# RMSNorm with swish: framework waits, 2 MB transfers, and stores moved to a second issuing engine

## The chip, the cores and the metric

The kernel runs on one core of a Trainium2 chip; the other cores are idle. The metric is the device time of the program in microseconds (us), as the median of several executions. A profile gives the time line of one execution; its span is about 1.8 us shorter than the device time of the same execution (165.0 against 166.75 us before). Engines: ACT is ScalarE, DVE is VectorE, POOL is GpSimd, SP is SyncE, which only issues transfers here. A letter q after the name (SPq, ACTq) means the engine's sequencer, which issues DMA transfers and waits on semaphores. A semaphore is a counter on which an engine waits. A packet is one record of a DMA engine in the trace; a data packet here is 8 KB in a 1 MB transfer and 16 KB in one of 2 MB. A load or store of a tile has landed when the last of its sixteen completion events is recorded.

## The reference

```python
x = randn(16, 1024, 512)  # float32;  gamma = ones(512);  eps = 1e-5
rms = np.sqrt(np.mean(x ** 2, axis=-1, keepdims=True) + eps)
x_norm = x / rms * gamma
return x_norm * (1.0 / (1.0 + np.exp(-x_norm)))
```

The tensor has 16,384 rows of 2 KB, 33.6 MB. Each byte is read once and written once, 67.1 MB in all. There are 128 partitions, so the kernel holds 128 rows as "one row per partition"; four rows per partition are a piece of 1 MB.

## The kernel before

All waits are written by hand. SyncE issues both loads and stores, 1 MB each, in one program order: eight loads, and then a store and a load in turn. ACT makes three of four sums of squares and the swish, DVE the fourth sum and the normalization, POOL the power of -0.5. The cuts are marked.

```python
n = 4; n_act = 3; lead = 8; slots = 20          # T = 32 pieces of 1 MB
xb = pool.tile([P, slots, n, D], fp32, name="xb")
ld = [tc.alloc_semaphore(f"ld{s}") for s in range(slots)]
st = [tc.alloc_semaphore(f"st{s}") for s in range(slots)]
# ... ten more semaphores
def load(t):
    if t >= slots:
        nc.sync.wait_ge(st[t % slots], 16 * (t // slots))
    nc.sync.dma_start(out=X(t), in_=xv[t]).then_inc(ld[t % slots], 16)
def store(t):
    nc.sync.wait_ge(s_swish, t + 1)
    nc.sync.dma_start(out=ov[t], in_=X(t)).then_inc(st[t % slots], 16)
# ...
with tc.tile_critical():
    for t in range(lead):
        load(t)
    for t in range(T):
        store(t)
        if t + lead < T:
            load(t + lead)
    # ... ACT, DVE and POOL programs
    for s in range(slots):                       # the closing waits
        nc.sync.wait_ge(st[s], 16 * ((T - 1 - s) // slots + 1))
```

## Time and profile before

The time is 166.93 us, the median of three runs (166.81 to 167.04).

| what | value | how to read it |
|---|---|---|
| DMA, one queue | 97.0% of 16 engines | the sixteen DMA engines are nearly never idle: they bind |
| ACT, DVE busy | 120.5 us, 112.0 us | of 165.0 us: neither binds |
| rate in mid-span | 427 GB/s | 67.1 MB at that rate take 157 us |
| first transfer issued, first data | 0.94 us, 1.95 us | from the trace |
| last landing | 162.47 us | the last store's completion |
| end of the program | 164.97 us | 2.50 us after the last landing |

From the page of the kernel before: the span, the DMA share and the rate in 40 equal slices of 4.1 us, and the queues (packets, MB, share of 16 engines' span).

```profile
span 165.0 us, 713 instructions
...
DMA  4999999999999999999999999999999999999990
GB/s 157 415 425 429 425 342 429 411 431 427 427 431 419 431 423 433 423 431 425 429 427 427 423 425 431 421 435 419 435 423 431 425 425 431 421 433 423 433 405 26
...
q1 hardware_dynamic: 9216, 67.11, 97.0%
q14 instruction: 5, 0.04, 0.1%
```

DMA stands at 9 tenths from the second slice to the last but one. (In the tables below the DMA share can come out just above 1, for the recorded times of the packets are added up.) The one slice with 342 GB/s is where the first stores meet the loads.

The table by stretches of the kernel before. The columns are: stretch and length in us, busy us of DVE, ACT and POOL (with counts), clock, DMA share, GB/s.

```profile
20.00:22.00 2.00, 1.89 (x6) 2.00 (x5) 0.66 (x1) 1.00 0.97 360
22.00:24.00 2.00, 2.00 (x4) 2.00 (x6) 0.78 (x1) 1.00 0.92 324
...
60.00:80.00 20.00, 14.04 (x28) 15.38 (x31) 5.76 (x4) 1.00 1.01 427
...
155.00:159.00 4.00, 0.00 (x0) 0.00 (x0) 0.00 (x0) 1.00 1.01 426
159.00:161.00 2.00, 0.00 (x0) 0.00 (x0) 0.00 (x0) 1.00 0.91 385
161.00:163.00 2.00, 0.00 (x0) 0.00 (x0) 0.00 (x0) 1.00 0.06 25
163.00:165.00 2.00, 0.00 (x0) 0.00 (x0) 0.00 (x0) 1.00 0.01 4
```

So some 4 us pass at the end in which almost nothing moves. The view of the output tensor's transfers gives the last store's start (152.3 us) and the shortest time to landing (10.2 us), which belongs to that last store: it landed at 162.5 us.

```profile
L79 SPq DMA_DIRECT2D out_dram<-xb x32: 332/344/348, 15.3 to 152.3; - x32
...
DMA to landing us min/median/max: 10.2/22.4/24.0
```

### The profile page before, as it was taken

What the parts mean: (1) busy time and instruction counts of PE and PEld (TensorE: products, weight loads), DVE (VectorE), ACT (ScalarE), POOL (GpSimd) and SP (SyncE); (2) the same over time, 40 slices, a digit from 0 to 9 for tenths busy, and PEclk for the clock granted to TensorE, in tenths of its full rate; (3) what the DMA queues carried; (4) which work ended last, traced back from release to release, by engine and by line L of the source; (5) the groups of instructions that cost most, each with busy time, mean ns of one, the idle gap of its engine ahead of it and who ended that gap; (6) DMA issues with size and microseconds to landing.
All of it is one profiled execution on the core that took longest, in us unless ns stands there. A gap on an engine that the chain in (4) does not pass through costs nothing.

```text
span 165.0 us, 713 instructions
## 1 busy us (share of the span) xinstructions
DVE 112.0 (68%) x226; ACT 120.5 (73%) x225; POOL 46.4 (28%) x38
## 2 busy tenths in 40 slices
DVE  0269999999996666786666776666876666784000
ACT  3488999999977977777977758877778977777000
POOL 1053334443333311333321233312333311330000
DMA  4999999999999999999999999999999999999990
GB/s 157 415 425 429 425 342 429 411 431 427 427 431 419 431 423 433 423 431 425 429 427 427 423 425 431 421 435 419 435 423 431 425 425 431 421 433 423 433 405 26
DMA packets 9229, 67.16 MB, mean 407 GB/s; under 512 B 1028, under 2 KB 1028, under 8 KB 1032
## 3 DMA queue, kind: packets, MB, share of 16 engines
q1 hardware_dynamic: 9216, 67.11, 97.0%
q14 instruction: 5, 0.04, 0.1%
q10 hardware_dynamic: 8, 0.01, 0.0%
HBM read 33.56 MB, written 33.55 MB: 407 GB/s over the span
## 4 chain that ended last, share of the span: by engine, by line
DMA 63%; ACT 17%; issue 6%; DVE 5%; SPq 1%
DMA xb<-in_x_dram 63%; ACT junk_a L86 12%; ACT xb L129 6%; DVE xb L121 5%; SPq L79 1%; SPq L75 0%; DVE aeps L107 0%; SPq L203 0%; SPq L131 0%
## 5 line engine op out<-in xcount | busy, mean ns | idle before, releaser
L121 DVE SCALAR_TENSOR_TENSOR xb<-xb,rstd,gamma_sb 128x512 f32<-128x512 f32 x128 | 87.4, 745 | 0.0
L86 ACT ACTIVATE junk_a<-xb 128x512 bf16<-128x512 f32 x96 | 59.2, 617 | 26.9 <-DMA xb<-in_x_dram 26.9
L114 POOL TENSOR_TENSOR rstd<-aeps,neg_half 128x4 f32<-128x4 f32 x32 | 45.7, 1427 | 99.4 <-DVE aeps L107 99.4
L129 ACT ACTIVATE xb<-xb 128x2048 f32<-128x2048 f32 x32 | 60.6, 1895 | 2.2 <-DVE xb L121 2.2
L97 DVE CUSTOM_DVE_ANT_0 junk_v<-xb 128x512 bf16<-128x512 f32 x32 | 22.0, 689 | 8.7 <-DMA xb<-in_x_dram 6.8
L107 DVE TENSOR_SCALAR aeps<-ms 128x4 f32<-128x4 f32 x32 | 5.4, 170 | 29.6 <-ACT junk_a L86 28.9
L86 ACT ACTIVATION_READ_ACCUMULATOR junk_a<-xb 128x1 f32 x96 | 17.9, 186 | 0.0
L146 ACT ACT_TABLE_LOAD x1 | 1.3, 1283 | 2.6 <-issue 2.6
L97 DVE DVE_READ_ACCUMULATOR2_ANT ms<- 128x1 f32 x32 | 2.6, 82 | 0.0
L162 DVE STREAM_SHUFFLE gamma_sb<-gamma 128x512 f32<-128x512 f32 x1 | 0.7, 717 | 0.0
L141 POOL MEMSET gamma<- 128x512 f32 x1 | 0.5, 524 | 0.5 <-PEq L203 0.5
L189 POOL MEMSET const-float32-0.0<- 128x1 f32 x1 | 0.1, 99 | 0.2 <-issue 0.2
L189 POOL MEMSET const-uint8-127<- 128x1 uint8 x1 | 0.1, 102 | 0.0
L147 POOL MEMSET neg_half<- 128x4 f32 x1 | 0.1, 102 | 0.0
L189 POOL MEMSET const-bfloat16-1.0<- 128x1 bf16 x1 | 0.1, 101 | 0.0
L189 POOL MEMSET const-float32-1.0<- 128x1 f32 x1 | 0.1, 98 | 0.0
L162 DVE LOAD_MASK_SELECT gamma_sb<-gamma x1 | 0.0, 13 | 0.0
## 6 DMA issues: line engine op xcount, KB each, us to landing
xb<-in_x_dram SPq DMA_DIRECT2D x32, 1024.0 KB, 23.2
out_dram<-xb SPq DMA_DIRECT2D x32, 1024.0 KB, 22.4
gamma<-in_gamma_dram ACTq DMA_DIRECT2D x1, 8.0 KB
```

What stands on the lines that cost most here:

```text
L79: nc.sync.dma_start(out=ov[t], in_=X(t)).then_inc(st[t % slots], 16)
L86: ins = nc.scalar.activation(out=junk_a[:, j, :], in_=X(t)[:, j, :], func=AF.Square, accum_out=ms[:, t, j : j + 1],)
L97: ins = nc.vector.tensor_tensor_reduce(out=junk_v[:, j, :], in0=X(t)[:, j, :], in1=X(t)[:, j, :], scale=1.0, scalar=0.0, op0=ALU.mult, op1 ...
L107: nc.vector.tensor_scalar(out=aeps[:, t, :], in0=ms[:, t, :], scalar1=inv_d, scalar2=eps_f, op0=ALU.mult, op1=ALU.add,).then_inc(s_aeps, 1)
L114: nc.gpsimd.tensor_tensor(out=rstd[:, t, :], in0=aeps[:, t, :], in1=neg_half[:], op=ALU.pow).then_inc(s_rstd, 1)
L121: ins = nc.vector.scalar_tensor_tensor(out=X(t)[:, j, :], in0=X(t)[:, j, :], scalar=rstd[:, t, j : j + 1], in1=gamma_sb[:], op0=ALU.mult, ...
L129: nc.scalar.activation(out=X(t), in_=X(t), func=AF.Silu).then_inc(s_swish, 1)
L141: nc.gpsimd.memset(gamma4[:], 0.0).then_inc(s_const, 1)
L146: nc.scalar.preload_act_table_set("silu_and_others")
L147: nc.gpsimd.memset(neg_half[:], -0.5).then_inc(s_half, 1)
L162: nc.vector.stream_shuffle(gamma_sb[:], gamma4[:], [0] * 32).then_inc(s_gamma, 1)
L189: nc = _bacc.Bacc("TRN2", target_bir_lowering=False, num_devices=1)
```

## The change

Its intent: let the framework set the waits, in the order in which the program is written; fewer and larger transfers; loads free to run ahead of stores, because each has a queue of its own. The diff, cut to its core (the compute instructions, their shapes and their order on ACT and DVE stay):

```diff
-    n = 4
-    lead = 8
-    slots = 20
+    sizes = [4, 4] + [8] * 15     # rows per partition of each transfer
+    ring = 96
+    ahead = 32
+    cn = 4                        # compute pieces stay 1 MB
-    ld = [...]; st = [...]        # and ten more semaphores: gone
     def load(t):
-        if t >= slots:
-            nc.sync.wait_ge(st[t % slots], 16 * (t // slots))
-        nc.sync.dma_start(out=X(t), in_=xv[t]).then_inc(ld[t % slots], 16)
+        nc.sync.dma_start(out=buf(t), in_=dram(xf, t))
     def store(t):
-        nc.sync.wait_ge(s_swish, t + 1)
-        nc.sync.dma_start(out=ov[t], in_=X(t)).then_inc(st[t % slots], 16)
+        nc.scalar.dma_start(out=dram(of, t), in_=buf(t))
-    with tc.tile_critical():
+    with tc.manual_schedule():
+        # ... loads until `ahead` rows are issued
+        for k in range(K + 3):
+            if k < K:
+                sums(k)
+                root(k)
+            while stored < len(tiles) and ends[stored] <= k - 2:
+                store(stored)
+                stored += 1
+            # ...
+            if 1 <= k <= K:
+                norm(k - 1)
+            if 2 <= k < K + 2:
+                swish(k - 2)
+                # ... further loads
-        for s in range(slots):
-            nc.sync.wait_ge(st[s], 16 * ((T - 1 - s) // slots + 1))
```

More of the change, by code (lines that the diff above doesn't have):

```diff
@@ L27 @@
     R, D = xf.shape
-    n = 4
+    sizes = [4, 4] + [8] * 15
+    ring = 96
+    ahead = 32
+    cn = 4
     n_act = 3
-    lead = 8
-    slots = 20
-    T = R // (P * n)
-    assert T * P * n == R, (R, n)
-    xv = xf.rearrange("(t p n) d -> t p n d", p=P, n=n)
-    ov = of.rearrange("(t p n) d -> t p n d", p=P, n=n)
+    N = sum(sizes)
+    assert N * P == R, (N, R)
+    tiles = []
+    done = 0
+    for sz in sizes:
+        assert done % ring + sz <= ring
+        tiles.append((done * P, sz, done % ring))
+        done += sz
@@ L39 @@
+    chunks = [r for _, sz, at in tiles for r in range(at, at + sz, cn)]
+    K = len(chunks)
     pool = ctx.enter_context(tc.tile_pool(name="all", bufs=1))
-    xb = pool.tile([P, slots, n, D], fp32, name="xb")
+    junk_pool = ctx.enter_context(tc.tile_pool(name="junk", bufs=1))
+    xb = pool.tile([P, ring, D], fp32, name="xb")
     gamma4 = pool.tile([P, D], fp32, name="gamma4")
     gamma_sb = pool.tile([P, D], fp32, name="gamma_sb")
-    junk_a = pool.tile([P, n, D], bf16, name="junk_a")
@@ L44 @@
-    junk_v = pool.tile([P, n, D], bf16, name="junk_v")
-    neg_half = pool.tile([P, n], fp32, name="neg_half")
-    ms = pool.tile([P, T, n], fp32, name="ms")
-    aeps = pool.tile([P, T, n], fp32, name="aeps")
-    rstd = pool.tile([P, T, n], fp32, name="rstd")
+    neg_half = pool.tile([P, cn], fp32, name="neg_half")
+    ms = pool.tile([P, K, cn], fp32, name="ms")
+    aeps = pool.tile([P, K, cn], fp32, name="aeps")
+    rstd = pool.tile([P, K, cn], fp32, name="rstd")
     inv_d = 1.0 / float(D)
@@ L51 @@
     eps_f = float(eps)
-    ld = [tc.alloc_semaphore(f"ld{s}") for s in range(slots)]
-    st = [tc.alloc_semaphore(f"st{s}") for s in range(slots)]
-    g_ld = tc.alloc_semaphore("g_ld")
-    s_const = tc.alloc_semaphore("s_const")
-    s_half = tc.alloc_semaphore("s_half")
-    s_gamma = tc.alloc_semaphore("s_gamma")
-    s_sum_a = tc.alloc_semaphore("s_sum_a")
-    s_sum_v = tc.alloc_semaphore("s_sum_v")
-    s_aeps = tc.alloc_semaphore("s_aeps")
-    s_rstd = tc.alloc_semaphore("s_rstd")
-    s_norm = tc.alloc_semaphore("s_norm")
@@ L64, with dram, buf @@
-    s_swish = tc.alloc_semaphore("s_swish")
-    def X(t):
-        return xb[:, t % slots]
-    def landed(eng, t):
-        eng.wait_ge(ld[t % slots], 16 * (t // slots + 1))
+    def dram(ap, t):
+        first, sz, _ = tiles[t]
+        return ap[first : first + P * sz].rearrange("(p n) d -> p n d", n=sz)
+    def buf(t):
+        _, sz, at = tiles[t]
+        return xb[:, at : at + sz, :]
     def load(t):
-        if t >= slots:
-            nc.sync.wait_ge(st[t % slots], 16 * (t // slots))
-        nc.sync.dma_start(out=X(t), in_=xv[t]).then_inc(ld[t % slots], 16)
+        nc.sync.dma_start(out=buf(t), in_=dram(xf, t))
@@ L77, in store @@
     def store(t):
-        nc.sync.wait_ge(s_swish, t + 1)
-        nc.sync.dma_start(out=ov[t], in_=X(t)).then_inc(st[t % slots], 16)
-    def sum_act(t):
-        landed(nc.scalar, t)
-        if t > 0:
-            nc.scalar.wait_ge(s_sum_a, t)
-        for j in range(n_act):
-            ins = nc.scalar.activation(
-                out=junk_a[:, j, :], in_=X(t)[:, j, :], func=AF.Square,
-                accum_out=ms[:, t, j : j + 1],
-            )
-        ins.then_inc(s_sum_a, 1)
-    def sum_dve(t):
-        landed(nc.vector, t)
-        if t > 0:
-            nc.vector.wait_ge(s_sum_v, t)
-        for j in range(n_act, n):
-            ins = nc.vector.tensor_tensor_reduce(
-                out=junk_v[:, j, :], in0=X(t)[:, j, :], in1=X(t)[:, j, :],
-                scale=1.0, scalar=0.0, op0=ALU.mult, op1=ALU.add,
-                accum_out=ms[:, t, j : j + 1],
-            )
-        ins.then_inc(s_sum_v, 1)
@@ L104, in mean_eps, with sums @@
-    def mean_eps(t):
-        nc.vector.wait_ge(s_sum_a, t + 1)
-        nc.vector.wait_ge(s_sum_v, t + 1)
+        nc.scalar.dma_start(out=dram(of, t), in_=buf(t))
+    def sums(k):
+        for j in range(cn):
+            row = xb[:, chunks[k] + j, :]
+            if j < n_act:
+                junk = junk_pool.tile([P, D], bf16, name=f"junk_a{j}")
+                nc.scalar.activation(
+                    out=junk[:], in_=row, func=AF.Square,
+                    accum_out=ms[:, k, j : j + 1],
+                )
+            else:
+                junk = junk_pool.tile([P, D], bf16, name=f"junk_v{j}")
+                nc.vector.tensor_tensor_reduce(
+                    out=junk[:], in0=row, in1=row,
+                    scale=1.0, scalar=0.0, op0=ALU.mult, op1=ALU.add,
+                    accum_out=ms[:, k, j : j + 1],
+                )
@@ L107, in mean_eps, with root @@
+    def root(k):
         nc.vector.tensor_scalar(
-            out=aeps[:, t, :], in0=ms[:, t, :], scalar1=inv_d, scalar2=eps_f,
+            out=aeps[:, k, :], in0=ms[:, k, :], scalar1=inv_d, scalar2=eps_f,
             op0=ALU.mult, op1=ALU.add,
-        ).then_inc(s_aeps, 1)
-    def root(t):
-        nc.gpsimd.wait_ge(s_aeps, t + 1)
+        )
         nc.gpsimd.tensor_tensor(
-            out=rstd[:, t, :], in0=aeps[:, t, :], in1=neg_half[:], op=ALU.pow
-        ).then_inc(s_rstd, 1)
-    def norm(t):
-        nc.vector.wait_ge(s_rstd, t + 1)
-        for j in range(n):
-            ins = nc.vector.scalar_tensor_tensor(
-                out=X(t)[:, j, :], in0=X(t)[:, j, :], scalar=rstd[:, t, j : j + 1],
+            out=rstd[:, k, :], in0=aeps[:, k, :], in1=neg_half[:], op=ALU.pow
+        )
@@ L123, in norm @@
+    def norm(k):
+        for j in range(cn):
+            row = xb[:, chunks[k] + j, :]
+            nc.vector.scalar_tensor_tensor(
+                out=row, in0=row, scalar=rstd[:, k, j : j + 1],
                 in1=gamma_sb[:], op0=ALU.mult, op1=ALU.mult,
             )
-        ins.then_inc(s_norm, 1)
-    def swish(t):
-        nc.scalar.wait_ge(s_norm, t + 1)
-        nc.scalar.activation(out=X(t), in_=X(t), func=AF.Silu).then_inc(s_swish, 1)
-    with tc.tile_critical():
-        for t in range(lead):
-            load(t)
-        for t in range(T):
-            store(t)
-            if t + lead < T:
-                load(t + lead)
-        nc.gpsimd.memset(gamma4[:], 0.0).then_inc(s_const, 1)
-        nc.scalar.wait_ge(s_const, 1)
-        nc.scalar.dma_start(
-            out=gamma4[0:P:32, :], in_=gamma.partition_broadcast(4)
-        ).then_inc(g_ld, 16)
-        nc.scalar.preload_act_table_set("silu_and_others")
-        nc.gpsimd.memset(neg_half[:], -0.5).then_inc(s_half, 1)
-        nc.gpsimd.wait_ge(s_half, 1)
-        for t in range(T + 2):
-            if t < T:
-                sum_act(t)
-            if t >= 2:
-                swish(t - 2)
-        for t in range(T + 1):
-            if t < T:
-                sum_dve(t)
-                mean_eps(t)
-            if t == 0:
-                nc.vector.wait_ge(g_ld, 16)
-                nc.vector.stream_shuffle(gamma_sb[:], gamma4[:], [0] * 32).then_inc(s_gamma, 1)
-            if t == 1:
-                nc.vector.wait_ge(s_gamma, 1)
-            if t >= 1:
-                norm(t - 1)
-        for t in range(T):
-            root(t)
-        for s in range(slots):
-            nc.sync.wait_ge(st[s], 16 * ((T - 1 - s) // slots + 1))
@@ new lines, in swish @@
+    def swish(k):
+        rows = xb[:, chunks[k] : chunks[k] + cn, :]
+        nc.scalar.activation(out=rows, in_=rows, func=AF.Silu)
+    with tc.manual_schedule():
+        nc.gpsimd.memset(gamma4[:], 0.0)
+        nc.gpsimd.memset(neg_half[:], -0.5)
+        nc.scalar.dma_start(out=gamma4[0:P:32, :], in_=gamma.partition_broadcast(4))
+        nc.scalar.preload_act_table_set("silu_and_others")
+        loaded = 0
+        rows_loaded = 0
+        while rows_loaded < ahead:
+            load(loaded)
+            rows_loaded += tiles[loaded][1]
+            loaded += 1
+        ends = []
+        e = 0
+        for _, sz, _ in tiles:
+            e += sz // cn
+            ends.append(e)
+        stored = 0
+        for k in range(K + 3):
[5 more added lines that the diff above has]
+                stored += 1
+            if k == 0:
+                nc.vector.stream_shuffle(gamma_sb[:], gamma4[:], [0] * 32)
+            if 1 <= k <= K:
+                norm(k - 1)
+            if 2 <= k < K + 2:
+                swish(k - 2)
+                while loaded < len(tiles) and ends[loaded] <= k - 1 + ahead // cn + 2:
+                    load(loaded)
+                    loaded += 1
```

## The prediction

> **What bounds the kernel now.** The DMA engines. The page's queue part gives one queue (q1) 67.11 MB and 97.0% of the 16 engines' span; the 40-slice part shows DMA at 9 tenths from slice 2 to slice 39 and about 427 GB/s, whether loads alone (slices 2 to 5) or loads and stores mixed. 67.1 MB at 427 GB/s is 157 us of the 165.0 us span. The rest: about 2.5 us until data flow, a dip to 342 GB/s in slice 6 (about 1 us, where the first stores meet the loads), and about 4 us after the last byte near 161 us (the table by stretches shows 49 GB/s in 161:162 and nothing after). ACT is busy 120.5 us and DVE 112.0 us, so neither binds: in the timeline a 1 MB piece costs ACT 3.64 us when it has data (sums start at 15.18, 18.81), and from about 40 us ACT waits for loads (26.9 us in the list of waits).
>
> **What the change does.** Bytes, arithmetic and its order on ACT and DVE stay. (a) Transfers of 2 MB: 16 KB rows instead of 8 KB and half the completions. One 8 KB packet takes 309 ns, in loads and stores alike; the Trainium skill, "DMA: Bandwidth & Descriptors", section on why small descriptors are slow, names a fixed cost of about 3 cycles per packet. If that halves, I estimate 0 to 1% of 157 us: 0 to 1.5 us gained. (b) Two queues: loads no longer stand behind stores in program order, and stores no longer behind loads. The same page, "Queues, rings and completion order", says each engine takes turns between queues by packet. Total bandwidth should not change; loads and stores should get about half each (213 GB/s) once both have work. That moves waits around under a DMA that is already 97% busy. (c) Store issue goes to ACT: 17 at about 0.35 us, about 6 us, off the bound except at the ends. (d) The first store comes later: the third chunk waits for a whole 2 MB load, and it comes after the fourth sum: about 20 us instead of 15.3 us. No loss, for loads fill the DMA. (e) The tail: after the last 2 MB load lands, ACT still has two sums (1.93 us each) and four swishes (1.9 us each) before the last store: about 12 us, then 2 MB at 427 GB/s (4.9 us) and 1 to 2 us of latency, 18 to 19 us in all. Hiding that needs about 8 MB of stores outstanding when loads end. An even split keeps loads about 7.4 MB ahead, so I estimate 0 to 2 us of idle DMA in the tail, against none now (152.3 us last issue, landing 10.2 us later).
>
> **Sum.** Minus 0 to 1.5 us (larger packets), plus 0 to 2 us (tail), the dip and the 4 us end unchanged: 166.0 us, practically the same. Range 163.6 to 169.0. Faster by over 2% 0.12, within 2% 0.77, slower by over 2% 0.11.
>
> **What would show it.** Right: two queues of 33.6 MB each; DMA 95 to 98% busy; 425 to 432 GB/s in mid-span; packets of 16 KB at 605 to 618 ns; last load lands near 138 to 144 us; ACT 119 to 123 us busy; a small gap of DMA in the last 20 us. Wrong: packets that get slower when the two queues mix, or a mid-span rate other than 420 to 435 GB/s.
>
> **What would make it wrong.** Stores favoured over loads: loads end late and the tail is exposed (170 us or more). The issue of stores blocking ACT for microseconds behind the loads' descriptors. Extra framework waits that serialise DMA and compute, or a longer end. For faster: 16 KB packets worth more than 1%, or a shorter start.

## More of the kernel before

The view of single source lines (durations in ns, minimum/median/maximum, then the first and the last start in us): L172 is the closing waits, L203 the end of the kernel.

```profile
L172 SPq EVENT_SEMAPHORE  x10: 17/28/28, 160.1 to 163.0; - x10
...
L203 SPq DRAIN  x3: 7/7/7, 163.9 to 164.2; - x3
...
L203 POOLq EVENT_SEMAPHORE_RANGE_CLEAR  x1: 333/333/333, 164.3 to 164.3; - x1
```

After the landing at 162.5 us the waits run on until 163.0 us, the drain comes at 163.9 us and the clearing of the semaphores at 164.3 us.

## The result

The changed kernel takes 163.88 us, the median of four runs (163.80 to 164.08), against 166.87 us for the kernel before in the same rounds. The ratio is 0.9822, 95% interval 0.9805 to 0.9839. Here and below a ratio is the mean time of one kernel's fast runs over that of the other's of the same rounds, so it is not quite the ratio of the medians. The kernel is 3.0 us faster: clear of the noise, just short of 2%, and more than three times the 0.9 us that was forecast.

The same parts of the page after the change:

```profile
span 162.1 us, 629 instructions
...
DMA  4999999999999999999999999999999999999992
GB/s 162 439 437 449 392 376 423 437 429 419 433 425 441 429 425 437 433 425 437 433 425 437 433 425 433 437 425 433 435 414 445 429 421 441 429 425 441 429 425 121
...
q1 hardware_dynamic: 2448, 33.56, 49.3%
q10 hardware_dynamic: 2456, 33.56, 48.4%
```

There are two queues with half of the bytes each, and the DMA is as busy as before. A slice is now 4.05 us, so the last slice holds fewer idle microseconds. The stretches after the change:

```profile
20.00:22.00 2.00, 2.00 (x5) 2.00 (x6) 0.30 (x1) 1.00 0.88 311
22.00:24.00 2.00, 1.78 (x6) 2.00 (x4) 1.44 (x1) 1.00 0.99 397
...
60.00:80.00 20.00, 6.84 (x14) 9.36 (x16) 2.88 (x2) 1.00 1.00 430
...
155.00:159.00 4.00, 0.00 (x0) 0.00 (x0) 0.00 (x0) 1.00 1.01 434
159.00:161.00 2.00, 0.00 (x0) 0.00 (x0) 0.00 (x0) 1.00 0.08 33
```

The rate is 430 instead of 427 GB/s; it holds to 159 us with no gap in the tail; the dip at 20 to 24 us is still there. The output transfers and the end of the program after the change:

```profile
L73 ACTq DMA_DIRECT2D out_dram<-xb x17: 338/338/357, 16.8 to 151.2; - x17
...
DMA to landing us min/median/max: 9.9/16.7/21.6
```

```profile
L178 SPq EVENT_SEMAPHORE  x7: 17/28/30300, 121.1 to 162.0; - x7
...
L178 SPq DRAIN  x3: 7/7/7, 161.3 to 161.6; - x3
...
L178 POOLq EVENT_SEMAPHORE_RANGE_CLEAR  x1: 95/95/95, 161.7 to 161.7; - x1
```

The last store lands at 151.2 + 9.9 = 161.1 us, and only 0.2 us later SP drains. The trace's records of single instructions, packets and completions give the sum of the 2.9 us of span to a hundredth:

| part | before | after | difference |
|---|---|---|---|
| first data packet at | 1.95 us | 1.74 us | -0.21 |
| first data to last landing | 160.52 us | 159.34 us | -1.18 |
| last landing to end | 2.50 us | 1.00 us | -1.50 |
| span | 164.97 us | 162.08 us | -2.89 |

More than half of the gain lies outside the data phase, in the frame of the program. Yet such a table only says where the time went. Whether larger packets, the second queue or the framework's waits brought it has to be tried.

### The profile page after: what moved, and what is told of

It reads as the page before. It is cut to its first block, busy times and chain, and to the rows that moved or that the text cites. A ratio compares the mean times of both kernels' runs of the same rounds, so it can differ in the third digit from the quotient of the medians.

```text
span 162.1 us, 629 instructions
## 1 busy us (share of the span) xinstructions
DVE 110.3 (68%) x226; ACT 118.8 (73%) x225; POOL 46.4 (29%) x38
## 3 DMA queue, kind: packets, MB, share of 16 engines
q1 hardware_dynamic: 2448, 33.56, 49.3%
q10 hardware_dynamic: 2456, 33.56, 48.4%
HBM read 33.56 MB, written 33.55 MB: 414 GB/s over the span
## 4 chain that ended last, share of the span: by engine, by line
DMA 47%; ACT 36%; issue 4%; DVE 3%; another core or an unknown queue 1%; SPq 0%; ACTq 0%; DVEq 0%
DMA xb<-in_x_dram 36%; ACT junk_a L80 19%; ACT xb L111 17%; DMA out_dram<-xb 12%; DVE xb L104 3%; SPq L70 0%; ACTq L73 0%; DVEq L178 0%; DVE aeps L93 0%; ACTq L80 0%
## 5 line engine op out<-in xcount | busy, mean ns | idle before, releaser
L111 ACT ACTIVATE xb<-xb 128x2048 f32<-128x2048 f32 x32 | 60.7, 1897 | 23.1 <-DMA xb<-in_x_dram 21.2
```

Of the source, the lines that this page charges most:

```text
L111: nc.scalar.activation(out=rows, in_=rows, func=AF.Silu)
```

## The experiments

Three theories were to be told apart. A: the larger packets shorten the data phase. B: the form of the program (framework waits, no hand-written closing waits, no critical section) shortens the start and the end, whatever the transfers are. C, the rival for the data phase: the second queue does it. The change has three parts, so six kernels give all the corners between before and after: hand-written or framework waits (h, f), one or two queues (1q, 2q), 1 or 2 MB. They ran with five rounds each. Their table, before the single stories; "end" is from the last landing to the end, "spread" the time between the first and the last of the sixteen completions of the last transfer, all read from the trace:

| kernel | time, us | ratio | data phase | end | spread |
|---|---|---|---|---|---|
| before (h, 1q, 1 MB) | 166.87 | 1 | 160.52 | 2.50 | 1.8 |
| h_1q_2mb | 166.78 | 1.0002 | 161.30 | 1.61 | 3.1 |
| h_2q_1mb | 166.43 | 0.9967 | 160.84 | 2.14 | 1.9 |
| h_2q_2mb | 164.72 | 0.9862 | 159.37 | 1.61 | 1.9 |
| f_1q_1mb | 164.73 | 0.9874 | 160.69 | 0.88 | 2.2 |
| f_1q_2mb | 165.49 | 0.9914 | 160.99 | 1.00 | 3.0 |
| f_2q_1mb | 173.15 | 1.0377 | 168.73 | 0.88 | 0.2 |
| after (f, 2q, 2 MB) | 163.88 | 0.9822 | 159.34 | 1.00 | 1.9 |

The phases come from one profile each and move by some 0.3 us from run to run; the ratios have intervals of about plus or minus 0.0015. Each ratio is taken against the kernel before in the same rounds, whose median was 166.87 or 166.97 us. Two profiles caught the slowest execution of their kernel: f_1q_1mb (0.35 us above its median) and h_2q_1mb (0.29 us above). Their data phases are to be read as about 0.3 us shorter. The data phase of f_2q_1mb is that of waits which are explained below; with them mostly out of the way (f_2q_1mb_ring44) it is 160.71 us.

### f_1q_1mb: the framework's waits alone

```diff
-    sizes = [4, 4] + [8] * 15
+    sizes = [4] * 32
-        nc.scalar.dma_start(out=dram(of, t), in_=buf(t))
+        nc.sync.dma_start(out=dram(of, t), in_=buf(t))
```

> The changed kernel with 1 MB transfers and with its stores issued from SyncE again: of the change only the framework's waits are left. Theory A (16 KB packets shorten the data phase by about 1.2 us) and theory B (the framework form starts 0.2 us earlier and ends 1.5 us sooner after the last landing) together say 165.2 us: all of B, nothing of A. Theory C (the second queue gives the gain) says 166.9 us, as before.

Measured: 164.73 us, ratio 0.9874 (0.9862 to 0.9887). That is 2.1 us less than before, with 8 KB packets at 309 ns, one queue and the data phase of before (160.69 against 160.52 us). The first transfer is issued at 0.74 us instead of 0.94, and the end takes 0.88 us instead of 2.50. Theory B is shown, and it is the larger part of the gain when it is taken first. Taken last, it is worth less: see h_2q_2mb.

### h_waits_in_order: what the end is made of

```diff
-        for s in range(slots):
+        for s in sorted(range(slots), key=lambda s: (T - 1 - s) // slots * slots + s):
             nc.sync.wait_ge(st[s], 16 * ((T - 1 - s) // slots + 1))
```

> The kernel before with its last 20 semaphore waits in the order in which the stores land, so that none is left after the last landing. Theory B in detail: before, about 9 wait instructions of 0.06 us ran after the last landing, so 0.5 us less: 166.4 us. If those waits hide behind something else in the closing barrier: 166.9 us.

Measured: 166.48 us, ratio 0.9969 (0.9954 to 0.9984), the end 1.95 us. In the kernel before, the last store belongs to slot 11, and the waits for slots 12 to 19 came behind it though all of them had long been met. The instruction records show nine wait instructions between 162.49 and 163.03 us; now there is one. So 0.5 us of the 1.5 us is the order of waits that wait for nothing. The rest can be read but was not tried alone: before, 0.9 us pass from the last wait (163.03 us) to the closing drain (163.92 us; a branch out of the critical section and the meeting of the engines lie between), 0.1 us after the change; and clearing the semaphores takes 333 ns for the many of the hand-written kernel and 95 ns for the few of the framework.

### h_1q_2mb: the larger transfers alone

```diff
-    n = 4; lead = 8; slots = 20
+    n = 4; lead = 5; ring = 80                  # lead 5 is still 32 rows
+    sizes = [4, 4] + [8] * 15                   # one ld and one st semaphore for each
 # ... pieces of 1 MB wait for ld[owner[t]]; a store waits for s_swish >= ends[i]
```

> The kernel before with 2 MB transfers (two of 1 MB first), hand-written waits, one queue, the same 1 MB compute pieces, 80 rows of buffer, 5 transfers of lead. A and B: 165.7 us, packets at 611 ns, mid-span 430 to 431 GB/s, last landing to end still about 2.3 us. C: 166.9 us.

Measured: 166.78 us, ratio 1.0002 (0.9984 to 1.0019); both theories miss something. The packets do take 611 ns, which is less than twice 309. But the data phase is not shorter; it is 0.8 us longer, although the closing waits became cheaper by the way (0.9 us less end: 0.5 us because all store semaphores are now waited for in the order of landing, and 0.3 us because SyncE's next instruction follows the branch after 0.16 instead of 0.43 us, for a reason that stays open). The packet records show what differs: after 45 us there are 45 packets that took over 8% longer than 611 ns, by 71 to 1089 ns, against 4 packets over 8% longer than 309 ns in the kernel before. They come in clusters every 9.8 us (45 to 47, 55 to 57, 64 to 67 us and so on), which is the period of one 2 MB load and one 2 MB store in the one queue, and a cluster has one to nine such packets, so it can't hit more than nine of the sixteen engines. The spread of the sixteen completions grows from 1.0 us at 44 us to 3.1 us at 120 us and stays. So some completions of a transfer fall behind the others and do not catch up: at the end the rate falls away from 159 us on, and the last completion comes at 163.26 us. That the delayed packets make the lag is read from these records and was not tried by itself.

### h_2q_1mb: the second queue alone

```diff
 def store(t):
-    nc.sync.wait_ge(s_swish, t + 1)
-    nc.sync.dma_start(...)
+    nc.scalar.wait_ge(s_swish, t + 1)
+    nc.scalar.dma_start(...)
-        for t in range(lead): ...               # SyncE: loads and stores in turn
+        for t in range(T):
+            load(t)                             # SyncE: loads only
 # ACT: store(t - 3) behind the sums of piece t, as in the change
```

> The kernel before with its stores issued from ScalarE and its loads from SyncE as far as the 20 slots allow; 1 MB transfers, hand-written waits. A and B: 166.9 us, no change. C (the second queue gives the gain): about 165.5 us.

Measured: 166.43 us, ratio 0.9967 (0.9955 to 0.9979). The data phase is not shorter (160.84 us in the profile against 160.52). The end is 0.36 us shorter (2.14 us), which is most of the 0.5 us of the ratio and lies outside the theories about the queue (0.28 us of it is again the stretch after the branch). The rest agrees with a data phase that did not change: this profile caught an execution of 166.72 us, 0.29 us above the median. Theory C by itself falls.

### h_2q_2mb: both, with hand-written waits

```diff
 # h_1q_2mb with store() on nc.scalar, and SyncE issuing the 17 loads alone
```

> The kernel before with both the second queue and 2 MB transfers, hand-written waits kept. A and B: 165.7 us, that is 1.7 us above the change, all of it in the start and after the last landing. If the framework's waits matter in the middle as well (its bound on transfers in flight), the data phase differs too.

Measured: 164.72 us, ratio 0.9862 (0.9848 to 0.9876). The data phase is 159.37 us, that of the change to 0.03 us, at 431 GB/s. After 45 us there are 2 long packets, and the spread is 1.9 us. So the data phase needs both parts: 2 MB transfers alone bring +0.8 us, the second queue alone nothing clear of what profiles differ by, both together -1.2. Neither A nor C was right alone. The ring here is still 80 rows, so the change's larger ring of 96 rows is not what shortens the data phase. With the second queue the order of issue changed too, for SyncE issues loads as far ahead as the ring allows; no run parts the queue from that order. The expected 165.7 us was 1.0 us too high because this version's end is also 0.9 us shorter than that of the kernel before. Put on top of this kernel, the framework's form brings only 0.8 us more (164.72 to 163.88 us). So its part in the gain is 2.1 us when it comes first and 0.8 us when it comes last: this kernel's rewritten hand-made waits had already taken 0.9 us off the end.

### f_1q_2mb: the change with one queue

```diff
-        nc.scalar.dma_start(out=dram(of, t), in_=buf(t))
+        nc.sync.dma_start(out=dram(of, t), in_=buf(t))
```

> The changed kernel with its stores issued from SyncE, one queue. A and B: 163.9 us, as the change. C: 165 us or more. Stores that stand behind loads in the one program order could leave gaps in the DMA; then it is slower than both say and the 40 slices show it.

Measured: 165.49 us, ratio 0.9914 (0.9901 to 0.9927). It confirms the pair of the last two from the other side: with one queue there are 33 long packets after 45 us, the spread is 3.0 us, and the data phase is 1.65 us longer than with two. The 40 slices show no gap behind the first stores' dip, so SyncE's program order did not starve the DMA. Compared with f_1q_1mb it is even slower by 0.8 us. Why a turn from one direction to the other in a queue costs something with 16 KB packets and not with 8 KB packets is open.

### f_2q_1mb: the change with 1 MB transfers

```diff
-    sizes = [4, 4] + [8] * 15
+    sizes = [4] * 32
```

> The changed kernel with 1 MB transfers, nothing else. A and B: 165.2 us, packets of 8 KB at 309 ns, mid-span 427 GB/s, last landing to end 1.0 us. C: about 164 us, as the change, for the second queue is still there.

Measured: 173.15 us, ratio 1.0377 (1.0363 to 1.0390). No theory had this. Its table by stretches (stretch, length, busy us of DVE, ACT and POOL with counts, clock, DMA share, GB/s) shows the DMA up to 30% idle at the end while ACT is busy all 10.00 us of each stretch, so ACT binds there:

```profile
120.00:130.00 10.00, 9.42 (x19) 10.00 (x22) 3.72 (x3) 1.00 1.01 428
130.00:140.00 10.00, 9.50 (x19) 10.00 (x19) 4.32 (x3) 1.00 0.88 368
140.00:150.00 10.00, 9.35 (x21) 10.00 (x20) 4.32 (x3) 1.00 0.75 310
150.00:160.00 10.00, 9.35 (x21) 10.00 (x22) 3.47 (x3) 1.00 0.70 288
```

ACT has the same work as ever, so it must have lost time earlier. Its list of waits (total us, times, longest):

```profile
ACT xb L111 <- DMA xb<-in_x_dram: 39.3, 9, 9.5
```

L111 is the swish, which has no reason to wait for a load: its data came long before. In the order of ACT's program a store stands just before it. The changed kernel has the same kind of wait (21.2 us in 4 waits), and its timeline shows one of them:

```profile
52.73 0.19 ACT L80 ACTIVATION_READ_ACCUMULATOR junk_a<-xb 128x1 f32 x1
60.66 0.34 ACTq L73 DMA_DIRECT2D out_dram<-xb  x1
61.04 1.91 ACT L111 ACTIVATE xb<-xb 128x2048 f32<-128x2048 f32 x1 [8.12 <-DMA xb<-in_x_dram]
```

ACT stood still from 52.9 to 60.6 us in front of a store. The records of the semaphores name the reason. The framework counts all transfers on eight counters in turn. This store counts on the one on which a load issued at 17.82 us had counted, and that load landed at 60.58 us; the store's extra wait ended then. ACT, a compute engine, thus waited for a load that neither the store nor the swish needed.

### f_2q_1mb_ring44: the same with the counters out of each other's way

```diff
     sizes = [4] * 32
-    ring = 96
+    ring = 44
```

> The changed kernel with 1 MB transfers (173.15 us) and a ring of 44 rows instead of 96, nothing else. Theory D: it was slow because the framework counts transfers on eight shared counters, and a store issued from ACT waited (up to 9.5 us, 39 us in all) until a load with the same counter had landed. With 44 rows loads and stores alternate in the framework's order, so from the sixth store on a store shares its counter with an earlier store alone: 165.2 to 165.6 us, no wait of ACT over 3 us after 50 us. Rival E: two queues with 1 MB packets starve the loads: still about 173 us or more, for the smaller ring only lets loads run less far ahead.

Measured: 165.14 us, ratio 0.9894 (0.9881 to 0.9908): 8.0 us less from a ring of less than half the size. Rival E falls, and theory D holds as far as this run can tell: ACT's waits for loads fell from 39.3 to 22.7 us. The smaller ring also keeps loads from running ahead while ACT stands still, and no run parts these two effects. The list of ACT's waits from 60 us on, for f_2q_1mb and then for this kernel:

```profile
ACT xb L111 <- DMA xb<-in_x_dram: 25.4, 6, 6.4
```

```profile
ACT xb L111 <- DMA xb<-in_x_dram: 9.1, 1, 9.1
ACT xb L111 <- DMA out_dram<-xb: 7.3, 6, 1.7
```

One detail of the expectation was wrong: it said that no wait of ACT would be over 3 us after 50 us, and two are. The eighth store (55.65 us) and the 23rd (127.34 us) still shared a counter with a load, which landed at 55.57 and at 127.27 us; ACT waited 5.2 and 9.1 us before the swishes behind them. The tenth to the 22nd store share their counters with stores and wait 1.7 us at most. In h_2q_1mb, where each slot has a semaphore of its own, there is no such wait at all.

### a_early_store: what the dip at 20 us is

```diff
         nc.scalar.dma_start(out=gamma4[0:P:32, :], in_=gamma.partition_broadcast(4))
+        nc.scalar.dma_start(out=of[0:P, 0:cn], in_=neg_half[:])
```

> The changed kernel with one tiny store more (128 rows of 16 bytes into rows that are stored again later), issued from ACT at about 2.5 us. If the dip at 18 to 24 us (about 0.9 us lost, packets of up to 1.2 us) is a cold first store on each engine: the dip is gone or smaller and the time 0.5 to 0.9 us less than the change, 163.0 to 163.4. If it comes from stores and loads meeting at all: no change, 163.9 us.

Measured: 164.34 us, ratio 0.9845 (0.9829 to 0.9862), against 164.01 us and 0.9828 (0.9814 to 0.9841) for the changed kernel on the same chip. There is no gain, and the dip stays: 336 and 377 GB/s in 20:22 and 22:24. A small early store does not take it away; what else makes it is open. The kernel before has it too, so it plays no part in the difference.

### a_4mb: packets of 32 KB

```diff
-    sizes = [4, 4] + [8] * 15
+    sizes = [4, 4, 8] + [16] * 6 + [8, 4, 4]
```

> The changed kernel with transfers of 4, 4, 8, six of 16, 8, 4, 4 rows, so packets of 32 KB. From 309 ns for 8 KB and 611 ns for 16 KB theory A makes it 7 ns fixed and 302 ns per 8 KB: 1215 ns, mid-span 433 GB/s, 0.5 to 0.7 us less than the change, 163.2 to 163.4 us. Against it: a store waits for 16 rows to be computed, and stores that wait on a load's counter could hold up ACT so long that the tail is exposed: then 165 us or more.

Measured: 163.08 us, ratio 0.9774 (0.9755 to 0.9793), faster than before by more than 2% and 0.9 us below the changed kernel; 0.5 to 0.7 us was expected. The 32 KB packets take 1213 ns, as expected. The data phase is 158.84 us, 0.6 us less than in the anchor run's 159.44 us, and the end is 0.87 us. ACT waits 30.0 us for loads, and the DMA stays at 9 tenths in all slices from the second to the last but one, except two at 8 tenths; so these waits cost little or nothing. This version beats both kernels.

### after_again: the anchor

The changed kernel unedited, on the chip of the last three.

> The changed kernel itself, once more, as the anchor on this chip for the two runs before it: 163.9 us, ratio 0.982.

Measured: 164.01 us (163.83 to 164.21), ratio 0.9828. It repeats the result.

## Why the prediction was right or wrong

What bounds the kernel was right: DMA before and after, and no gain came from ACT or DVE.

The step that failed is "the dip and the 4 us end unchanged". The dip did stay. The end did not: from the last landing on it shrank from 2.50 to 1.00 us, and the start from 0.94 to 0.74 us. These 1.7 us were a term of zero in the sum. The prediction read the last microseconds as time after the last byte, and its text names no instruction that stands in them; among what would make it wrong it lists "a shorter start" and "a longer end", but not a shorter end. The lines L172 and L203 of the profile before show ten waits and the closing drain there, and the diff takes both the waits and the critical section away. The framework's waits alone, f_1q_1mb, gave 2.1 of the 3.0 us; on top of the other two parts they gave 0.8.

The number itself does not follow from the prediction's own terms. Minus 0 to 1.5 and plus 0 to 2 from 166.9 us is 165.4 to 168.9 us, with its middle at 167.1, not 166.0. So no choice within the stated terms reaches the measured 163.88 us, and that this time lies just inside the stated range of 163.6 to 169.0 owes nothing to the terms.

The second mis-sized term is the tail, put at plus 0 to 2 us. It measured 0: the rate is 434 GB/s up to 159 us. The estimate put the loads 7.4 MB ahead of the stores when they ended, near 138 to 144 us, and wanted about 8 MB. Loads and stores did share evenly while both had work: 2.14 MB of loads and 2.17 MB of stores in 60 to 70 us. But while stores were short of work, loads took the engines: 5.25 against 3.01 MB in 20 to 40 us, and, while ACT stood before a shared counter, 3.39 against 0.92 MB in 70 to 80 us. So the last packet of the loads' queue started at 131.6 us, and 11.9 MB of stores were left to hide the last computations behind. The blocked stores, which the prediction had listed as a danger ("extra framework waits"), were not needed for that: in h_2q_2mb, without shared counters, the loads' last packet started at 137.9 us with 9.2 MB of stores left, and there is no gap in the tail either (434 GB/s from 150 to 158 us). So the lead of the loads was mis-sized. With 1 MB transfers and the large ring the shared counters cost 8 us.

The packet term, minus 0 to 1.5 us, was right in size: the data phase fell by 1.2 us. Twice 309 less 611 ns is 7 ns for each packet saved; a DMA engine moves 512 data packets before and 272 after, so 240 fewer are worth 1.7 us by this estimate. Its reason was incomplete. As h_1q_2mb shows, larger packets bring it only together with the second queue. "Total bandwidth should not change" with two queues holds for 8 KB packets (h_2q_1mb) and fails for 16 KB packets, where one queue has a data phase longer by 1.9 us (h_1q_2mb against h_2q_2mb).

The predicted signs came true in most parts: two queues of 33.56 MB, mid-span 430 to 433 GB/s, packets of 611 ns, ACT 118.8 us busy (119 to 123 was said). Three did not: the last load landed at 133.2 us and not at 138 to 144, the first store was issued at 16.8 us and not at about 20, and there was no DMA gap in the last 20 us before the last store's data ended.

## What to carry to other kernels

In a kernel that a full DMA binds, look at the instructions between the last landing and the end before you size a change: closing waits, a critical section and many semaphores were together worth 1.5 us of 167 here, of which 0.5 us (the order of the waits) was tried alone. Judge transfer size and the number of queues together, for 2 MB transfers in one queue of turning directions gained nothing, and in two queues they gained 1.2 us. If a framework counts transfers on a few shared counters, find out which earlier transfer each store of a compute engine has to wait for; that wait was free at 2 MB and cost 8 us at 1 MB with a ring of 96 rows.

## What the Trainium skill lacked or had wrong

- "DMA: Bandwidth & Descriptors", "Issuing engines are not separate DMA queues", says that issuing from several engines saves sequencer time only. With 8 KB packets the runs agree (data phase 160.84 us with two queues, 160.52 with one). With 16 KB packets they don't: 159.37 us with two queues and 161.30 with one, where 45 packets after 45 us took 71 to 1089 ns longer, in clusters at the period of one load and one store.
- The same page, "Why small descriptors are slow", names a fixed overhead of about 3 cycles per packet and calls it worth joining descriptors into packets at 256 B or less only. Longer rows are another step, which it does not size. Here packets of 8, 16 and 32 KB took 309, 611 and 1213 ns, which is about 302 ns per 8 KB and 7 ns fixed, and with two queues the data phase was 159.37 us with 16 KB and about 160.5 us with 8 KB (160.84 us in a profile that was 0.29 us slow).
- The same page, "Queues, rings and completion order", on engines taking turns between queues, is not contradicted: 2.14 against 2.17 MB in 60 to 70 us while both had work.
- "Runtime: NRT & Kernel Launch", "Instruction fetch mechanics", does not say what a fetch costs data transfers that are under way. In the kernel before, fetches of 8 KB (in the queue named instruction) fall at 31.9, 32.0, 93.9 and 104.7 us. The spread of the sixteen completions of a transfer steps up beside the first three, from 0.7 to 1.2 us and from 1.1 to 1.9 us, and does not come back; beside the fourth it stays. In the kernel before, h_2q_1mb, h_2q_2mb and the changed kernel each fetch from 45 us to the end of the data (two in every kernel) is followed 0.31 us later, when its own 309 ns are over, by the start of a long data packet. That fetches cause the steps is read from the coincidence and was not tried.
- No page was found that sizes a program's own end after its last landing: 2.50 us in the kernel before, 1.61 us with hand-written waits in order and fewer semaphores, 0.87 to 1.08 us with the framework's waits.
